# Level masks on VectorE, a residual loaded in eight pieces and a gate bank emptied by ScalarE, in a transformer trunk layer on one core

## The chip, the cores and the metric

The kernel runs on one core of one Trainium2 chip. The metric is the device time of one execution in microseconds (us); the number for a kernel is the median of several runs. Engines are named as in the profile: PE (TensorE), DVE (VectorE), ACT (ScalarE), POOL (GpSimd) and SP (SyncE, which issues the DMAs).

## The reference

One layer of a streaming encoder for two request groups, 256 + 64 = 320 tokens in all, width 2048:

```
h = rmsnorm(x);  p = h @ w_in                       # 2048 -> 6160 columns
a_out = conformer_conv(p[:, :2048])                 # GLU, depthwise conv of width 31, group norm, swish
b_out = gdn_mixer(p[:, 2048:])                      # 8 heads of gated delta rule, chunks of 64 tokens
x = x + rmsnorm(concat(a_out, b_out) @ w_out)
h = rmsnorm(x)
gu = causal_dwconv(h @ w_up)                        # 2048 -> 11264, width 3
x = x + rmsnorm((silu(gate) * up) @ w_down)         # 5632 -> 2048
```

The delta rule of a chunk needs the inverse of a triangular matrix `m + eye`:

```
m = where(strict, einsum('bhnid,bhnjd->bhnij', kb, k) * decay, 0.0)
tmat = triangular_solve(m + eye, eye, lower=True, unit_diagonal=True)
```

All of it is float32, and the states of the convolutions and of the delta rule are returned as well.

## The kernel before

Activations lie with channels on the 128 partitions and the 320 tokens in the free dimension. Every float32 operand of a large product is split into a high and a low part, and each weight tile gives three matmuls into one PSUM bank (high x high, high x low, low x high: L210, L211 and L214 of `block_matmul`). The weights are streamed: `load_split` has SP start the DMA of one piece of up to 128x1024 elements into one of three buffers `w`, ACT casts it into `whi` (L194), and DVE subtracts to get `wlo` (L195). There are three buffers each for `w`, `whi` and `wlo`, so a DMA starts when the piece three before it has been split.

PE runs the dense products as one long row, and everything else hangs on it. Small pieces of work are generators, called jobs: the gates, the tail of a convolution block, the tail of a head, and a pair of heads with its triangular inverse. `tick` is called after each dense matmul, and after every 20 it takes the jobs that are due in order and advances each by one step, as long as the PSUM banks of pool g (four banks) and pool t (two banks) that their steps ask for, summed within the tick, don't exceed 4 and 2. A step's instructions are then put behind that matmul; the framework's scheduler makes one fixed order for each engine out of this.

`levels` joins the inverse of 16-wide diagonal blocks (which `base_inverse` made) into 32-wide and then 64-wide blocks. It runs four times, once for each pair of heads, and has two masked levels, w=16 and w=32. N (tile `np`) is the factor; a level takes only its blocks right above the block diagonal. Before, POOL multiplies N by a 0/1 mask into `nm` (L720), PE forms `pz` from `nm` (L729), ACT copies `pz` to `zs` (L730), and PE forms `px` and `py` from `zs` (L734, L737), which DVE adds to the inverse `wtp` (L738, L739). This is done for all NI = 5 chunks of two heads at once, so the tiles have 128x640 (nm) or 128x320 (zs, px, py) elements.

`gates` empties the bank `psba` (the raw gates of the 8 heads, in pool p) with two DVE products with `rb`, the row of reciprocal norms (L398, L399). The bank is one of the two that the dense products alternate on.

After the mixer the second dense product with `w_out` runs in two parts; the last is a loop over 16 blocks n, each with one piece `w_out2[n]` of 320 KB, 15 matmuls and the sum of squares. The residual x is loaded into `x1` (2.56 MB, L932) ahead of this loop, followed by the parameters `fpar` (L933). `x1` is first read after the loop.

Of the kernel before, what the change touches and what calls it, by code (L numbers as in the profile page):

```python
# [9 lines left out]
F32 = mybir.dt.float32  # L10
F32R = mybir.dt.float32r
AF = mybir.ActivationFunctionType
ALU = mybir.AluOpType
# [4 lines left out]
P = 128  # L18
D = 2048
KB = D // P  # L20
TP = 256
TS = 64
# [57 lines left out]
def chunk_constants():  # L80
    i = np.arange(P)
    c = np.zeros((P, NCST), np.float32)

    def put(name, m):
        o, w = CST[name]
        c[:, o:o + w] = m

    put("ident", np.eye(P))
    put("tri", i[:, None] <= i[None, :])
    put("strict", i[:, None] > i[None, :])  # L90
    put("ones", 1.0)
    same = i[:, None] // TS == i[None, :] // TS
    put("tri2", same & (i[:, None] <= i[None, :]))
    put("strict2", same & (i[:, None] > i[None, :]))
    put("half", 0.5)
    for name, b in (("m16", 16), ("m32", 32)):
        r, q = i[:, None] // b, i[None, :] // b
        put(name, (r % 2 == 0) & (q == r + 1))
    return c


# [1 line left out]
def trunk_kernel(ctx, tc, ins, outs):  # L103
# [7 lines left out]


    dense = [None, 0]
    jobs = []


# [8 lines left out]
    def advance(job):  # L125
        with tc.issue_after(dense[0]), tc.high_priority(offset=PRI_J):
            try:
                wait, job[2], job[3] = next(job[1])
                job[0] = dense[1] + wait
            except StopIteration:  # L130
                jobs.remove(job)
# [10 lines left out]
    def tick(mm):  # L142
        dense[0] = mm.ins
        dense[1] += 1
        if dense[1] % GAP == 0:
            g = t = 0
            for job in sorted(jobs, key=lambda j: j[0]):
                if job[0] <= dense[1] and g + job[2] <= 4 and t + job[3] <= 2:
                    g += job[2]
                    t += job[3]  # L150
                    advance(job)
            for _ in range(min(pace[0], len(taps))):
                next_tap()

# [240 lines left out]

    def gates():
        baT = cb.tile([32, 3, P], F32, tag="un", bufs=1, name="baT").rearrange("p c f -> p (c f)")
        V.tensor_tensor(baT[:, 0:T], psba[0:32, 0:T], rb[0:32, :], ALU.mult)  # L398
        V.tensor_tensor(baT[:, T:T + TS], psba[0:32, TP:T], rb[0:32, TP:T], ALU.mult)  # L399
        ba = const.tile([P, 3, 16], F32, tag="ba", name="ba")  # L400
        yield LAG_WAIT, 0, 1
        pst = ps_t.tile([P, 512], F32, tag="t", name="pst_ba")
# [313 lines left out]
    def levels(st):  # L716
        N, W, TT = st["np"], st["w"][:, 0, :, :], st["w"][:, 1, :, :]
        for name, w in (("m16", 16), ("m32", 32)):
            nm = gd.tile([P, NI, P], F32, tag="nm", bufs=1, name="nm")
            G.tensor_tensor(nm, N, cv(name).unsqueeze(1).to_broadcast((P, NI, P)), ALU.mult)  # L720
            G.memset(halves(zs, 16, 1) if w == 16 else halves(zs, w, 1)[:, :, :, 0:16], 0.0)
            pz, px, py = [], [], []

            def out(name):
                return ps_g.tile([P, 512], F32, tag="g", name=name)[:, 0:NI * 64].rearrange("p (a b w) -> p a b w", a=NI, w=w)

            pz = out("pz")
            for a in range(NI):
                PE.matmul(pz[:, a], nm[:, a, :], halves(TT, w, 0)[:, a], start=True, stop=True)  # L729
            S.copy(halves(zs, w, 0), pz)  # L730
            yield LAG_WAIT, 2, 0
            px, py = out("px"), out("py")
            for a in range(NI):
                PE.matmul(px[:, a], zs[:, a, :], halves(W, w, 1)[:, a], start=True, stop=True)  # L734
            nt = NI if w == 16 else S_
            for a in range(nt):
                PE.matmul(py[:, a], W[:, a, :], halves(zs, w, 0)[:, a], start=True, stop=True)  # L737
            V.tensor_tensor(halves(W, w, 1), halves(W, w, 1), px, ALU.add)  # L738
            V.tensor_tensor(halves(TT, w, 0)[:, 0:nt], halves(TT, w, 0)[:, 0:nt], py[:, 0:nt], ALU.add)  # L739
            yield LAG_ADD, 1, 0  # L740
        pz = ps_g.tile([P, 512], F32, tag="g", name="pz")[:, 0:256].rearrange("p (a f) -> p a f", a=S_)
        for a in range(S_):
            PE.matmul(pz[:, a, :], N[:, a, :], TT[:, a, 0:64], start=True, stop=True)
        S.copy(zs[:, 0:S_, 0:64], pz)
        yield LAG_WAIT, 1, 0
        px = ps_g.tile([P, 512], F32, tag="g", name="px")[0:64, 0:256].rearrange("p (a f) -> p a f", a=S_)
        for a in range(S_):
            PE.matmul(px[:, a, :], zs[:, a, 0:64], W[:, a, 64:128], start=True, stop=True)
        S.copy(W[0:64, 0:S_, 64:128], px)
# [179 lines left out]
    x1 = res.tile([P, KB, T], F32, tag="x1", name="x1")  # L929
    fpar = res.tile([P, NFP], F32, tag="fpar", name="fpar")  # L930
    nffn = res.tile([P, 88, 2, 2], F32, tag="nffn", name="nffn")
    nc.sync.dma_start(x1, ins["x"])  # L932
    nc.sync.dma_start(fpar, ins["fpar"])  # L933
    acc = None

    def fv(name, a, b=None):
# [24 lines left out]
    for n in range(KB):  # L961
        hi, lo = load_split(ins["w_out2"][n], nk2 * P)
        if n in (4, 8):
            upw.append(up_weights(len(upw), ugp))
        whole = n == KB - 1
        psm = ps_p.tile([P, 512], F32, tag="p", name="psm2")
        if whole:
# [257 lines left out]
```

## Time and profile before

| | |
|---|---|
| median of 3 runs | 1529.96 us (1528.54 to 1530.36) |
| the profiled execution, its own time | 1527.28 us |
| its span, first to last instruction | 1525.2 us |
| mean granted TensorE clock | 0.997 of full speed |
| PE busy | 1502.0 us (98%), 10232 matmuls |
| DVE busy | 1009.9 us (66%) |
| ACT busy | 734.4 us (48%) |
| POOL busy | 303.6 us (20%) |
| DMA moved | 224.29 MB, mean 147 GB/s |

The profile is one execution, taken apart into instructions. Busy is the time in which an engine has an instruction in work; the rest of the span it waits. The times in the sections below count from the start of the span. The 2 us between span and own time lie before the first and after the last instruction.

### The profile page before, as it was taken

To read this page: it belongs to the slowest core of one execution; us is meant where nothing else is said; L and a number is where in the kernel's file an instruction comes from. 1 tells how busy PE (TensorE), PEld (TensorE's weight loads), DVE (VectorE), ACT (ScalarE), POOL (GpSimd) and SP (SyncE) were. 2 spreads that over 40 slices of the span, in tenths; PEclk is the share of its full clock that TensorE was granted. 3 is DMA by queue.
4 is the path that set the end of the run, shared out by engine and by line. 5 is a ranking of instruction groups with operands and counts; after the bars stand their busy time and mean duration, and the time that the engine had idled before them with its cause. 6 is when DMAs were issued, how large, how long until landed. Compare 5 with 4: busy or idle time off the path is not lost.

```text
span 1525.2 us, 26534 instructions
## 1 busy us (share of the span) xinstructions
PE 1502.0 (98%) x10232; PEld 1480.9 (97%) x10232; DVE 1009.9 (66%) x1841; ACT 734.4 (48%) x1215; POOL 303.6 (20%) x475
## 2 busy tenths in 40 slices
PE   9999999989999999999999999999999999999998
PEld 8999999989999989999999999999999999999997
DVE  6679797888997469766435665545666545666554
ACT  7674655545555565544334444333444333444453
POOL 0323233331110000332001322101222101222101
PEclk9999999999999999999999999999999999999999
DMA  8435443444434653444455455455544455444453
GB/s 297 129 112 159 143 142 110 119 146 119 132 101 138 202 169 125 140 151 144 134 152 168 150 153 149 126 151 170 153 152 149 128 152 167 151 152 152 127 151 116
DMA packets 95974, 224.29 MB, mean 147 GB/s; under 512 B 18536, under 2 KB 36968, under 8 KB 95720
## 3 DMA queue, kind: packets, MB, share of 16 engines
q1 hardware_dynamic: 95704, 222.57, 48.4%
q8 instruction: 80, 1.31, 0.4%
q14 instruction: 46, 0.38, 0.1%
q10 hardware_dynamic: 144, 0.03, 0.0%
HBM read 215.45 MB, written 7.12 MB: 146 GB/s over the span
## 4 chain that ended last, share of the span: by engine, by line
PE 86%; DVE 9%; ACT 1%; issue 1%; POOL 1%; DMA 1%; DVEq 0%; ACTq 0%; SPq 0%; POOLq 0%
PE psu L210 13%; PE psu L211 13%; PE psu L214 13%; PE psdn L210 7%; PE psdn L211 7%; PE psdn L214 7%; DVE cvt L513 3%; DVE wlo L195 3%; PE psq L210 2%; PE psq L211 2%; PE psq L214 2%; PE psm L214 1%; PE psm L211 1%; PE ps_first L372 1%; PE psm L210 1%
## 5 line engine op out<-in xcount | busy, mean ns | idle before, releaser
L194 ACT CAST whi<-w 128x1024 fp32r<-128x1024 f32 (+2 forms) x440 | 413.0, 940 | 509.0 <-PE psu L211 171.3
L195 DVE TENSOR_TENSOR wlo<-w,whi 128x1024 fp32r<-128x1024 f32 (+2 forms) x440 | 478.0, 1087 | 184.7 <-ACT whi L194 106.0
L210 PE MATMUL psu<-hi,whi 128*128 128x320 f32 x1344 | 397.0, 309 | 1.3 <-DVE fbuf L1062 1.3
L211 PE MATMUL psu<-lo,whi 128*128 128x320 f32 x1344 | 396.9, 309 | 0.0
L210 PEld LDWEIGHTS psu<-hi,whi 128*128 128x128 f32 x1344 | 252.3, 188 | 1.4 <-ACT rb L1044 1.4
L211 PEld LDWEIGHTS psu<-lo,whi 128*128 128x128 f32 x1344 | 252.3, 188 | 0.0
L214 PE MATMUL psu<-hi,wlo 128*128 128x320 f32 x1344 | 224.4, 309 | 0.0
L1063 POOL COPY nffn<-fbuf 128x2 f32<-128x2 f32 x88 | 101.4, 1153 | 588.4 <-DVE fbuf L1061 584.0
L211 PE MATMUL psdn<-gl,whi 128*128 128x320 f32 x704 | 208.9, 310 | 0.0
L214 PEld LDWEIGHTS psu<-hi,wlo 128*128 128x128 f32 x1344 | 204.1, 188 | 0.0
L210 PE MATMUL psdn<-gh,whi 128*128 128x320 f32 x512 | 152.3, 309 | 0.0
L1061 DVE TENSOR_TENSOR fbuf<-psu,rb 128x256 f32<-128x256 f32 x88 | 37.3, 424 | 169.8 <-PE psu L214 169.8
L513 DVE SCALAR_TENSOR_TENSOR cvt<-ub,par,cvt 128x350 f32<-128x350 f32 x240 | 141.1, 602 | 2.7 <-ACT cvt L512 0.3
L211 PEld LDWEIGHTS psdn<-gl,whi 128*128 128x128 f32 x704 | 132.2, 188 | 0.3
L210 PE MATMUL psq<-hh,whi 128*128 128x320 f32 x352 | 106.5, 316 | 1.2 <-DVE baT L399 1.2
L211 PE MATMUL psq<-hl,whi 128*128 128x320 f32 x352 | 104.1, 309 | 0.0
L210 PEld LDWEIGHTS psdn<-gh,whi 128*128 128x128 f32 x512 | 96.1, 188 | 0.0
L214 PE MATMUL psdn<-gh,wlo 128*128 128x320 f32 x512 | 95.8, 309 | 0.0
L214 PEld LDWEIGHTS psdn<-gh,wlo 128*128 128x128 f32 x512 | 80.4, 188 | 0.0
L210 PEld LDWEIGHTS psq<-hh,whi 128*128 128x128 f32 x352 | 66.1, 188 | 1.8 <-issue 1.6
L211 PEld LDWEIGHTS psq<-hl,whi 128*128 128x128 f32 x352 | 66.2, 188 | 0.3 <-issue 0.2
L1105 DVE TENSOR_TENSOR y<-y,psdn 128x320 f32<-128x320 f32 x48 | 23.4, 488 | 63.6 <-PE psdn L214 63.6
(328 smaller groups left out, 2514.0 us busy)
## 6 DMA issues: line engine op xcount, KB each, us to landing
w<-in_w_up SPq DMA_DIRECT2D x176, 512.0 KB, 3.7
w<-in_w_in SPq DMA_DIRECT2D x88, 512.0 KB, 3.7
w<-in_w_down SPq DMA_DIRECT2D x64, 384.0 KB, 3.0
w<-in_w_down SPq DMA_DIRECT2D x64, 320.0 KB, 2.8
w<-in_w_out SPq DMA_DIRECT2D x32, 320.0 KB, 2.9
w<-in_w_out SPq DMA_DIRECT2D x16, 384.0 KB
w<-in_w_first SPq DMA_DIRECT2D x6, 512.0 KB, 5.5
wtp<-wsp SPq DMA_DIRECT2D x4, 640.0 KB
```

What stands on the lines that cost most here:

```text
L194: S.copy(hi[:, 0:width], w[:, 0:width])
L195: V.tensor_tensor(lo[:, 0:width], w[:, 0:width], hi[:, 0:width].bitcast(F32), ALU.subtract)
L210: tick(PE.matmul(ps, wh, xh, start=(k0 + j == 0), stop=False))
L211: tick(PE.matmul(ps, wh, xl, start=False, stop=False))
L214: tick(PE.matmul(ps, lo[:, j * P:(j + 1) * P], xh, start=False, stop=(final and k0 + j == nk - 1)))
L372: tick(PE.matmul(ps, w, xh, start=(k == 0 and wt is hi), stop=(k == KB - 1 and wt is lo)))
L513: return lambda: V.scalar_tensor_tensor(cvt, ub[:, t:t + 350], pv("w_dw", b * 31 + t), cvt, ALU.mult, ALU.add)
L1061: V.tensor_tensor(buf[:, 2:258], psu[:, 0:TP], rb2[:, 0:TP], ALU.mult)
L1063: G.tensor_copy(nffn[:, b, 0, :], buf[:, 256:258])
L1105: V.tensor_tensor(y[:, n, :], y[:, n, :], psd[:, 0:T], ALU.add)
```

## The change

There are four edits. In `levels` the product on POOL goes away: PE multiplies the unmasked N, and DVE multiplies the product `pz` by the mask while it moves it to `zs`; ACT no longer copies it. The masks m16 and m32 are transposed for this. In `gates` two ACT copies take `psba` to SBUF at once, and one tick later DVE multiplies there by `rb`. In `tick` the pool-t banks asked for in the previous tick count against the limit too (`held_t`). And the residual is loaded in eight pieces of 320 KB, one in each of the first eight passes of the `w_out2` loop, with `fpar` in the tenth.

```diff
--- before.py
+++ after.py
@@ -95,7 +95,7 @@
     put("half", 0.5)
     for name, b in (("m16", 16), ("m32", 32)):
         r, q = i[:, None] // b, i[None, :] // b
-        put(name, (r % 2 == 0) & (q == r + 1))
+        put(name, (q % 2 == 0) & (r == q + 1))
     return c
 
 
@@ -111,6 +111,7 @@
 
 
     dense = [None, 0]
+    held_t = [0]
     jobs = []
 
 
@@ -143,12 +144,14 @@
         dense[0] = mm.ins
         dense[1] += 1
         if dense[1] % GAP == 0:
-            g = t = 0
+            g, t0 = 0, held_t[0]
+            t = t0
             for job in sorted(jobs, key=lambda j: j[0]):
                 if job[0] <= dense[1] and g + job[2] <= 4 and t + job[3] <= 2:
                     g += job[2]
                     t += job[3]
                     advance(job)
+            held_t[0] = t - t0
             for _ in range(min(pace[0], len(taps))):
                 next_tap()
 
@@ -395,8 +398,11 @@
 
     def gates():
         baT = cb.tile([32, 3, P], F32, tag="un", bufs=1, name="baT").rearrange("p c f -> p (c f)")
-        V.tensor_tensor(baT[:, 0:T], psba[0:32, 0:T], rb[0:32, :], ALU.mult)
-        V.tensor_tensor(baT[:, T:T + TS], psba[0:32, TP:T], rb[0:32, TP:T], ALU.mult)
+        S.copy(baT[:, 0:T], psba[0:32, 0:T])
+        S.copy(baT[:, T:T + TS], psba[0:32, TP:T])
+        yield 1, 0, 0
+        V.tensor_tensor(baT[:, 0:T], baT[:, 0:T], rb[0:32, :], ALU.mult)
+        V.tensor_tensor(baT[:, T:T + TS], baT[:, T:T + TS], rb[0:32, TP:T], ALU.mult)
         ba = const.tile([P, 3, 16], F32, tag="ba", name="ba")
         yield LAG_WAIT, 0, 1
         pst = ps_t.tile([P, 512], F32, tag="t", name="pst_ba")
@@ -716,8 +722,6 @@
     def levels(st):
         N, W, TT = st["np"], st["w"][:, 0, :, :], st["w"][:, 1, :, :]
         for name, w in (("m16", 16), ("m32", 32)):
-            nm = gd.tile([P, NI, P], F32, tag="nm", bufs=1, name="nm")
-            G.tensor_tensor(nm, N, cv(name).unsqueeze(1).to_broadcast((P, NI, P)), ALU.mult)
             G.memset(halves(zs, 16, 1) if w == 16 else halves(zs, w, 1)[:, :, :, 0:16], 0.0)
             pz, px, py = [], [], []
 
@@ -726,8 +730,9 @@
 
             pz = out("pz")
             for a in range(NI):
-                PE.matmul(pz[:, a], nm[:, a, :], halves(TT, w, 0)[:, a], start=True, stop=True)
-            S.copy(halves(zs, w, 0), pz)
+                PE.matmul(pz[:, a], N[:, a, :], halves(TT, w, 0)[:, a], start=True, stop=True)
+            mask = cv(name).rearrange("p (b e w) -> p b e w", e=2, w=w)[:, :, 0, :]
+            V.tensor_tensor(halves(zs, w, 0), pz, mask.unsqueeze(1).to_broadcast((P, NI, P // 2 // w, w)), ALU.mult)
             yield LAG_WAIT, 2, 0
             px, py = out("px"), out("py")
             for a in range(NI):
@@ -929,8 +934,6 @@
     x1 = res.tile([P, KB, T], F32, tag="x1", name="x1")
     fpar = res.tile([P, NFP], F32, tag="fpar", name="fpar")
     nffn = res.tile([P, 88, 2, 2], F32, tag="nffn", name="nffn")
-    nc.sync.dma_start(x1, ins["x"])
-    nc.sync.dma_start(fpar, ins["fpar"])
     acc = None
 
     def fv(name, a, b=None):
@@ -962,6 +965,10 @@
         hi, lo = load_split(ins["w_out2"][n], nk2 * P)
         if n in (4, 8):
             upw.append(up_weights(len(upw), ugp))
+        if n < 8:
+            nc.sync.dma_start(x1[:, 2 * n:2 * n + 2, :], ins["x"][:, 2 * n:2 * n + 2, :])
+        elif n == 9:
+            nc.sync.dma_start(fpar, ins["fpar"])
         whole = n == KB - 1
         psm = ps_p.tile([P, 512], F32, tag="p", name="psm2")
         if whole:
```

The first place is DVE's order at pair 2's first level (w=16), some 326 us into the span. `gnm` belongs to a convolution's group norm, `cq` and `cvt` are accumulations of the short and the wide convolution. Before:

```order
L581 SCALAR_TENSOR_TENSOR cq<-qb_595,par,cq 128x323
L536 SCALAR_TENSOR_TENSOR gnm<-gvar,grs 128x3
L195 TENSOR_TENSOR wlo<-w,whi 128x1024
L581 SCALAR_TENSOR_TENSOR cq<-qb_595,par,cq 128x323
L513 SCALAR_TENSOR_TENSOR cvt<-ub_588,par,cvt 128x350
L195 TENSOR_TENSOR wlo<-w,whi 128x1024
L513 SCALAR_TENSOR_TENSOR cvt<-ub_588,par,cvt 128x350 x4
L738 TENSOR_TENSOR wtp<-wtp,px 128x20x16
L739 TENSOR_TENSOR wtp<-wtp,py 128x20x16
```

After the change (lines count three to six more there):

```order
L587 SCALAR_TENSOR_TENSOR cq<-qb_595,par,cq 128x323
L542 SCALAR_TENSOR_TENSOR gnm<-gvar,grs 128x3
L198 TENSOR_TENSOR wlo<-w,whi 128x1024
L587 SCALAR_TENSOR_TENSOR cq<-qb_595,par,cq 128x323
L735 TENSOR_TENSOR zs<-pz,cst 128x20x16
L198 TENSOR_TENSOR wlo<-w,whi 128x1024
L519 SCALAR_TENSOR_TENSOR cvt<-ub_588,par,cvt 128x350 x4
L743 TENSOR_TENSOR wtp<-wtp,px 128x20x16
L744 TENSOR_TENSOR wtp<-wtp,py 128x20x16
```

The product into `zs` now stands on DVE behind `gnm`, one `wlo` and one `cq`; one `cvt` that stood among them has moved down. On ACT the copy stood behind the `un` that `gnm` releases, two activations on `cq` (`vT`, `vts`) and a third `un`. Before, ACT had there:

```order
L539 ACTIVATE un<-pt_c,gnm,grs 128x128 x2
L582 ACTIVATE vT<-cq 128x256
L583 ACTIVATE vts<-cq 128x64
L539 ACTIVATE un<-pt_c,gnm,grs 128x128
L730 COPY zs<-pz 128x20x16
L194 CAST whi<-w 128x1024
```

The row `zs<-pz` is the one that has left ACT.

The second place is SP's queue of DMA issues at the residual load. Before, with `x_6072` the residual:

```order
L187 DMA w<-in_w_out 128x640 x6
L932 DMA x_6072<-in_x 128x5120
L187 DMA w<-in_w_up 128x4x256
L187 DMA w<-in_w_out 128x640 x2
L933 DMA fpar<-in_fpar 128x528
L187 DMA w<-in_w_out 128x640 x2
L187 DMA w<-in_w_up 128x4x256
L187 DMA w<-in_w_out 128x640 x7
```

After the change, where `x_6058` is the residual:

```order
L190 DMA w<-in_w_out 128x640 x6
L969 DMA x_6058<-in_x 128x640
L190 DMA w<-in_w_up 128x4x256
L969 DMA x_6058<-in_x 128x640 x2
L190 DMA w<-in_w_out 128x640
L969 DMA x_6058<-in_x 128x640
L190 DMA w<-in_w_out 128x640 x2
L969 DMA x_6058<-in_x 128x640
L190 DMA w<-in_w_out 128x640
L969 DMA x_6058<-in_x 128x640
L190 DMA w<-in_w_up 128x4x256
L190 DMA w<-in_w_out 128x640
```

The one large issue has become eight, which stand between the pieces of `w_out2`; the second piece of `w_up` has moved up among them, and the last two pieces of the residual and then `fpar` follow below these rows.

The third place is PE's order some 474 us into the span, where a convolution's second transposes (`pt_c<-cst,un`) take a bank of pool t that `pt_o` held. `psm` is the dense product. Before, 20 rows stand between `pt_o` and `pt_c`, and the last of them are:

```order
L214 MATMUL psm<-bh_4638,wlo 128x320
L214 MATMUL psm<-bh_5085,wlo 128x320
L214 MATMUL psm<-bp_2707,wlo 128x320
L210 MATMUL psm<-bp_2707,whi 128x320
L543 MATMUL pt_c_5512<-cst,un 128x128 x3
L211 MATMUL psm<-bl_2717,whi 128x320
```

After the change 38 rows stand between them, and the last are:

```order
L214 MATMUL psm<-bl_2270,whi 128x320
L213 MATMUL psm<-bh_3146,whi 128x320
L214 MATMUL psm<-bl_3147,whi 128x320
L213 MATMUL psm<-bh_4090,whi 128x320
L214 MATMUL psm<-bl_4091,whi 128x320
L549 MATMUL pt_c_5531<-cst,un 128x128 x3
L213 MATMUL psm<-bh_4628,whi 128x320
```

The transposes have moved down by 18 dense matmuls.

## Rows read from the trace of the kernel before

**Rows 1.** Windows: length, busy us (instructions) by engine, PEclk, DMA share, GB/s.

```profile
0.00:20.00 20.00, 18.66 (x103) 15.56 (x104) 13.19 (x20) 15.68 (x25) 2.50 (x7) 1.00 0.92 326
320.00:340.00 20.00, 14.80 (x88) 14.53 (x87) 16.02 (x32) 7.76 (x14) 3.78 (x7) 0.83 0.34 102
400.00:440.00 40.00, 39.33 (x293) 38.73 (x292) 38.38 (x71) 19.23 (x31) 5.12 (x6) 1.00 0.35 103
640.00:1500.00 860.00, 860.00 (x5858) 858.91 (x5857) 485.92 (x786) 367.93 (x487) 155.86 (x237) 1.00 0.50 149
```

**Rows 2.** Waits of PE, whole span: us in total, times, longest.

```profile
PE px L734 <- ACT zs L730: 5.9, 2, 5.2
...
PE pt_c L543 <- DVE zo L860: 2.0, 1, 2.0
...
PE psm L211 <- DVE bl L219: 1.1, 1, 1.1
...
PE psm L972 <- ACT whi L194: 0.5, 1, 0.5
```

**Rows 3.** Timeline at 326 us: start, us, engine, line, out<-in, count [idle <-releaser].

```profile
327.36 1.53 POOL L720 TENSOR_TENSOR nm<-np,cst 128x640 f32<-128x640 f32 x1
...
327.42 1.49 DVE L536 SCALAR_TENSOR_TENSOR gnm<-gvar,grs 128x3 f32<-128x3 f32 x1 [1.09 <-POOL grs L534]
...
328.83 1.21 DVE L195 TENSOR_TENSOR wlo<-w,whi 128x1024 fp32r<-128x1024 f32 x1
...
329.97 0.54 DVE L581 SCALAR_TENSOR_TENSOR cq<-qb,par,cq 128x323 f32<-128x323 f32 x1
...
331.36 0.41 ACT L730 COPY zs<-pz 128x320 f32<-128x320 f32 x1
...
331.82 2.40 PE L734 MATMUL px<-wtp,zs 128*128 128x64 f32 x10 [5.20 <-ACT zs L730]
...
334.01 2.34 PE L737 MATMUL py<-zs,wtp 128*128 128x64 f32 x10
...
336.11 2.38 PE L214 MATMUL psgate<-hh,wlo 128*128 128x320 f32 x8
```

**Rows 4.** Timeline elsewhere: the same PE work and the same gnm.

```profile
164.15 1.28 PE L737 MATMUL py<-zs,wtp 128*128 128x64 f32 x10
...
424.31 0.16 DVE L536 SCALAR_TENSOR_TENSOR gnm<-gvar,grs 128x3 f32<-128x3 f32 x1 [1.02 <-POOL grs L534]
```

**Rows 5.** Groups by line and form: busy, mean ns | idle before, releaser.

```profile
L720 POOL TENSOR_TENSOR nm<-np,cst 128x640 f32<-128x640 f32 x8 | 13.8, 1726 | 14.4 <-PE pz L729 7.6 <-DVE np L665 6.8
...
L738 DVE TENSOR_TENSOR wtp<-wtp,px 128x320 f32<-128x320 f32 x8 | 3.8, 478 | 4.4 <-PE py L737 4.4
```

**Rows 6.** Timeline at the emptying of the gate bank.

```profile
40.81 0.32 PE L285 MATMUL psba<-hl,wbz 128*128 128x320 f32 x1
...
47.49 1.33 PE L214 MATMUL psq<-hh,wlo 128*128 128x320 f32 x8
...
49.98 0.39 PE L210 MATMUL psq<-hh,whi 128*128 128x320 f32 x1 [1.16 <-DVE baT L399]
```

**Rows 7.** Timeline at the residual load.

```profile
523.86 0.33 SPq L932 DMA_DIRECT2D x<-in_x  x1
...
534.09 1.05 ACT L194 CAST whi<-w 128x1024 fp32r<-128x1024 f32 x1
...
536.41 0.41 PE L972 MATMUL psm<-bh,whi 128*128 128x320 f32 x1 [1.70 <-DVE wlo L195]
```

**Rows 8.** Windows while the residual landed, columns as in rows 1.

```profile
526.00:534.00 8.00, 8.00 (x57) 8.00 (x56) 4.88 (x9) 5.14 (x10) 0.00 (x0) 1.00 0.98 398
```

**Rows 9.** DMA issues of the page: KB each, us to landing.

```profile
w<-in_w_out SPq DMA_DIRECT2D x32, 320.0 KB, 2.9
```

**Rows 10.** Timeline at pair 3's first level.

```profile
404.61 1.81 DVE L513 SCALAR_TENSOR_TENSOR cvt<-ub,par,cvt 128x350 f32<-128x350 f32 x3
...
405.22 1.22 PE L734 MATMUL px<-wtp,zs 128*128 128x64 f32 x10
```

## The prediction

> **What bounds the kernel now.** I read the windows first. From 640 to 1500 us PE is busy in all 860 of 860 us [rows 1]: the change has nothing to win there, and all of its gain must come from the first third of the span and the stretch around the residual load. In the window from 320 to 340 PE is busy for only 14.80 us, and its granted clock is 0.83 [rows 1]: that is the one place ahead of the tail where the clock falls. The waits of PE say what stops it [rows 2]: `px` waits 5.9 us in all for ACT's `zs`, 5.2 of it at once; `pt_c` waits 2.0 for DVE's `zo`; `psm` waits 1.1 for DVE's `bl` and 0.5 for a cast. Two more stand in the timelines: 1.16 for DVE's `baT` [rows 6], and 1.70 at the residual load [rows 7]. Every one of these is touched by the change, and together they are 11 us plus the slower clock. So the question is not whether the edits aim at waits, but how much of each wait comes back.
>
> **The mask: the wait at 326 us.** In the timeline of pair 2's first level [rows 3] read backwards from `px` at 331.82. ACT's copy to `zs` runs at 331.36, behind activations that wait for `gnm` and `cq` of DVE. DVE's `gnm`, an instruction on 128x3 elements, begins at 327.42 and takes 1.49 us; the same `gnm` takes 0.16 at 424.31 [rows 4]. The difference, 1.33 us, lies exactly beside POOL's `nm` (327.36, 1.53 us). So POOL's product holds up a DVE instruction that reads two operands from SBUF, and that product is removed.
>
> After the change `zs` is DVE's, behind `gnm`, a `wlo` and a `cq`. I walk these from the rows: `wlo` starts 1.33 earlier than 328.83, at 327.50; `cq` 1.33 earlier than 329.97, at 328.64, and ends at 329.18; `zs` then takes about what the nearest row of its kind takes, a DVE addition of a PSUM bank of 128x320 to SBUF, 478 ns [rows 5]. So `zs` is done at 329.66, and `px` starts near 329.7 instead of 331.82: 2.1 us come back. Pair 2's other `nm` product goes as well, and if it holds DVE up by another 1.33 at a time when DVE has no slack, up to 3.4 come back; nothing less than 2.1 does unless the DVE queue grows. I take 2.5, nearer the walk. A wait of about 2.7 stays.
>
> **The mask: the clock at 326 us.** Behind the wait of 5.20 us PE runs at a lower clock: `px` and `py`, ten matmuls each, take 2.40 and 2.34 us, and the eight of `psgate` behind them 2.38 [rows 3]. The same `py` takes 1.28 at 164.15 [rows 4], and eight matmuls of that form 1.33 at 47.49 [rows 6]. The loss is 2.40 + 2.34 - 2 x 1.28 = 2.2, and 2.38 - 1.33 = 1.0, so 3.2 us. The window's 0.83 agrees: 17% of 20 us, 3.4. After the residual load's wait of 1.70 the clock was not lost, nor after the 2.0 of `pt_c`: the windows show it in this one place only. A wait of 2.7 lies between 2.0, where it stays at 2.4 GHz, and 5.2, where it goes to 1.2; being nearer to the first, I take all 3.2, with 0 as the other bound.
>
> **The mask: the rest.** DVE gains eight `zs` of 0.48 us, 3.8 us in all, and loses what `nm` costs it. POOL's eight products take 1.73 us each [rows 5]; where DVE stands beside one with two SBUF operands it can lose up to 1.33, eight times 10.6 at the most. Either way DVE is not loaded more than before by more than 3.8 us. That matters because DVE is busy 38.38 of 40 us between 400 and 440 [rows 1]. At pair 3's first level `px` starts at 405.22 without a wait, while DVE runs three `cvt` from 404.61 to 406.42 [rows 10]; a `zs` that stands inside such a run comes some 0.3 to 0.6 us late. I give back 0.4 there, and allow 1.4 for all the other small leads of weight pieces that the earlier PE eats into (0.5 at each of three places, estimated from `zs`' own 0.48). ACT loses eight short copies, and it is not what PE waits for; they are worth nothing.
>
> **The gate bank.** The last product into it ends at 41.13, and PE needs the bank again after the eight matmuls at 47.49, that is at 48.82, but starts at 49.98, having waited 1.16 [rows 6]: DVE's products stand behind others that need `rb`. The two ACT copies need no `rb`, and have over seven us for less than one (the copy of 128x320 on ACT takes 0.41 [rows 3]). The whole 1.2 comes back.
>
> **The limit on pool-t banks.** `pt_c` moves down by 18 matmuls. At 0.15 us each that is 2.6 us, more than the wait of 2.0, so the bank is free when PE comes to it. But DVE loses the breath that the wait gave it, and what reads `pt_c` moves down as well. I take 1.6, between 0 and 2.0. The `bl` of the 1.1 us wait comes a little earlier on DVE: 0.6, between 0 and 1.1.
>
> **The residual.** The single load begins at 523.86 on SP's queue [rows 7], and from 526 to 534 the queues run at 398 GB/s [rows 8]; the pieces of weights behind it land late: the next cast is at 534.09, and PE waits 1.70 to 536.41 [rows 7], and then 0.5 more [rows 2]. In eight pieces each pass of the loop asks for 320 KB of weights and 320 KB of residual, 655 KB. A pass has 15 matmuls, 2.2 us. So the demand is 298 GB/s, under the 398 shown here and the 326 that the start of the kernel sustains [rows 1]. I take all of 1.7 + 0.5 = 2.2, between 0 and 2.2.
>
> The Trainium skill's page "DMA: Bandwidth & Descriptors" (section "Bandwidth", the measured table's rule) speaks against this edit: batch DMAs to at least 1 MiB, since smaller ones don't reach three quarters of the peak; and its section "Anatomy of one DMA" gives a fixed cost of about 2.0 us a DMA. By its fit one load of 2.6 MB is about 8 us and eight of 320 KB are 22, an estimate, 14 more. The trace does not agree that pieces run one behind the other: at the start of the kernel, where x and the first weights come in pieces too, 326 GB/s were moved [rows 1].
>
> **The sum.** 1.2 + 2.5 + 3.2 + 0.6 + 1.6 + 2.2 = 11.3, less 1.8 given back, is 9.5 us. The profiled execution took 1527.28 us, so 1517.8 by its measure. The median of before is 1529.96, 2.7 above that execution; on it the same gain gives 1520.5.
>
> **The rivals.** *The clock falls again.* A wait of 2.7 may be long enough. Then the 3.2 are not won: 1523.7. For it speaks that nothing between 2.0 and 5.2 has been seen.
>
> *DVE takes the gain back.* From 400 to 440 DVE is nearly full [rows 1], and a stretch that DVE limits ends when DVE does, however early PE arrives. Then the gains ahead of it, 1.2 + 2.5 + 3.2 = 6.9, vanish, and the time is 1527.4. Against it: DVE's work follows PE's products, and can start earlier with them.
>
> *`zs` becomes the late one (slower).* ACT had room for the copy; DVE's queue in pairs 2 and 3 is full, with `wlo` of 1.21 and three `cvt` of 1.81 us ahead [rows 3, 10]. If `zs` waits behind 1.2 + 1.8 = 3.1 us at the three other levels of these pairs and at pair 2's first nothing is won in its walk, it is 3 x 3.1 + 2.5 above the forecast: 1532.3. It decides as soon as `px` waits over 3 us at two levels. Against it: the order puts `zs` behind a few rows only, and in front of most `cvt`.
>
> *Eight pieces run one after another.* A piece of 320 KB takes 2.9 us from issue to landing [rows 9]. If one piece of weights and one of residual landed in turn, a pass would take 5.8 instead of 2.2, eight times 3.6 = 29, less the lead of three buffers, 6.6; with the 2.2 not won it is 24 above the forecast, 1545. This is what the page's rule would do at its worst. Against it stand the 398 GB/s.
>
> **How the numbers follow.** Forecast 0.50, its own range 1517 to 1523.5 (all bounds won; the residual and 1 us more lost); clock 0.15; given back 0.14; `zs` late 0.08; pieces in turn 0.04; better than the forecast's range 0.09. This kernel's measurement tells 0.2%, 3 us, from no change, so faster is under 1526.9: 0.50 + 0.15 + 0.09 = 0.74; same 0.14; slower 0.12. The range reaches from 1516 to 1528: it leaves out the two slow cases and part of the best.
>
> **What the profile would show.** Right: no wait of `psq` for `baT`; no POOL product, and a `gnm` of 0.16 us at 326; `px` there waits near 2.7 us for DVE's `zs`, with the granted clock of 320 to 340 at 1.00; `pt_c` without a wait at 474; no wait of `psm` for weights at 536. Wrong: a window with a clock under 1, `px` waiting at several levels, or casts in the `w_out2` loop that wait for their DMA. What would upset all of it is a new wait in the stretch from 395 to 480, where DVE is late already.

## The result and the profile after

The changed kernel takes 1519.71 us (median of 4 runs, 1519.58 to 1520.18), the kernel before 1529.84 in runs beside it (4 runs, 1528.54 to 1530.36). The ratio is 0.9936 with a 95% interval of 0.9918 to 0.9953: it is faster by 0.5 to 0.8%. The forecast was 1520.5, with a range of 1516 to 1528.

The profiled executions differ by less than the medians do. After, span 1517.6 and own time 1520.18; before, 1525.2 and 1527.28. That is 7.6 us of span and 7.1 of own time against 10.1 us of median, and the difference is a finding of its own (below).

Answering to [rows 2], these are waits of PE in the changed kernel (us in total, times, longest):

```profile
PE px L739 <- DVE zs L735: 3.1, 2, 2.5
...
PE psm L979 <- DVE m L987: 1.2, 1, 1.2
...
PE pks L663 <- ACT vh L655: 1.0, 1, 1.0
...
PE psm L213 <- ACT whi L197: 1.0, 2, 0.7
...
PE psm L979 <- ACT whi L197: 0.9, 1, 0.9
```

Gone are `psq` for `baT`, `psm` for `bl` and `pt_c` for `zo`. The wait of `px` is 3.1 instead of 5.9. New or longer are a wait of `psm` for a sum `m` on DVE, `pks` for ACT (0.7 before, now 1.0), and `psm` for casts at three places, 455, 486 and 526 us.

Answering to [rows 1], windows of the changed kernel, with the stretch of the residual load as the third:

```profile
320.00:340.00 20.00, 17.46 (x109) 17.21 (x108) 14.79 (x32) 8.50 (x23) 4.97 (x10) 0.83 0.36 109
400.00:440.00 40.00, 39.40 (x295) 38.79 (x294) 38.40 (x74) 19.68 (x36) 3.62 (x5) 1.00 0.31 95
518.00:526.00 8.00, 7.89 (x54) 7.62 (x52) 4.17 (x7) 4.42 (x7) 0.00 (x0) 1.00 0.89 288
640.00:1500.00 860.00, 860.00 (x5858) 858.90 (x5857) 483.31 (x779) 367.10 (x486) 154.10 (x233) 1.00 0.49 148
```

PE is as full from 640 on as before, and the gain is all in front of it, as it had to be. PE has 17.46 of the 20 us from 320 to 340 instead of 14.80, but the granted clock of that window is 0.83 once more. DVE between 400 and 440 is as full as it was.

Answering to [rows 3], the timeline at pair 2's first level:

```profile
324.96 0.16 DVE L542 SCALAR_TENSOR_TENSOR gnm<-gvar,grs 128x3 f32<-128x3 f32 x1 [1.09 <-POOL grs L540]
...
325.04 1.22 DVE L198 TENSOR_TENSOR wlo<-w,whi 128x1024 fp32r<-128x1024 f32 x1
...
326.17 0.55 DVE L587 SCALAR_TENSOR_TENSOR cq<-qb,par,cq 128x323 f32<-128x323 f32 x1
...
326.64 0.48 DVE L735 TENSOR_TENSOR zs<-pz,cst 128x320 f32<-128x320 f32 x1
...
327.26 2.37 PE L739 MATMUL px<-wtp,zs 128*128 128x64 f32 x10 [2.54 <-DVE zs L735]
...
329.43 2.34 PE L742 MATMUL py<-zs,wtp 128*128 128x64 f32 x10
...
331.53 2.48 PE L217 MATMUL psgate<-hh,wlo 128*128 128x320 f32 x8
```

`gnm` takes 0.16 us, nothing stands on POOL beside it, and `zs` on DVE takes 0.48. PE's wait is 2.54. But `px`, `py` and the eight `psgate` run at 2.37, 2.34 and 2.48 us, as slowly as before, against 1.28 for the ten and 1.33 for the eight at full clock [rows 4, 6].

Answering to [rows 7], the stretch of the residual in eight pieces:

```profile
523.49 1.05 ACT L197 CAST whi<-w 128x1024 fp32r<-128x1024 f32 x1 [1.38 <-DMA w<-in_w_up]
...
526.01 0.72 ACT L197 CAST whi<-w 128x640 fp32r<-128x640 f32 x1 [0.50 <-DMA w<-in_w_out]
...
526.74 0.39 PE L979 MATMUL psm<-bh,whi 128*128 128x320 f32 x1 [0.85 <-ACT whi L197]
...
535.14 1.68 ACT L197 CAST whi<-w 128x1024 fp32r<-128x1024 f32 x2 [1.26 <-DMA w<-in_w_up]
...
538.50 0.48 DVE L987 TENSOR_TENSOR m<-m,psm 128x320 f32<-128x320 f32 x1
...
539.13 0.38 PE L979 MATMUL psm<-bh,whi 128*128 128x320 f32 x1 [1.16 <-DVE m L987]
```

ACT's cast of a piece of `w_up` (L197, 128x1024) comes late because its DMA lands late; what stands behind it on ACT and DVE is late with it, and PE waits twice: 0.85 for a cast, 1.16 for DVE's sum `m`, which frees a bank. So 2.0 us of new waits stand where 1.7 and 0.5 stood.

Of the 7.6 us of span, the waits that can be named on both sides come to 6.2: gate bank 1.16, a gate wait of 0.3 behind it, `px` 2.66 in pair 2 and 0.07 net in pair 3, `bl` 1.06, `pt_c` 1.96 and the residual 0.22, less 0.34, 0.30 and 0.66 for the longer waits of `pks` and of casts at 455 and 486. That is all of PE's idle time: span less PE's busy time is 23.2 us before and 17.0 after. The other 1.4 us are PE's busy time (1502.0 before, 1500.6 after), and I did not assign them to rows.

### The profile page after: what moved, and what is told of

The parts are those of the page before. It is cut to its first block, busy times and chain, and to the rows that moved or that the text cites. A ratio compares the mean times of both kernels' runs of the same rounds, so it can differ in the third digit from the quotient of the medians.

```text
span 1517.6 us, 26528 instructions
## 1 busy us (share of the span) xinstructions
PE 1500.6 (99%) x10231; PEld 1480.4 (98%) x10232; DVE 1007.1 (66%) x1849; ACT 732.4 (48%) x1209; POOL 286.9 (19%) x467
## 4 chain that ended last, share of the span: by engine, by line
PE 90%; DVE 6%; ACT 1%; POOL 1%; issue 1%; DMA 1%; ACTq 0%; DVEq 0%; POOLq 0%
PE psu L213 13%; PE psu L214 13%; PE psu L217 13%; PE psdn L213 7%; PE psdn L214 7%; PE psdn L217 7%; PE psq L217 3%; PE psq L213 3%; PE psq L214 3%; DVE wlo L198 2%; DVE cvt L519 2%; PE ps_first L375 1%; PE psu L1034 1%; PE psm L213 1%; PE psm L214 1%; PE psv L217 1%
## 5 line engine op out<-in xcount | busy, mean ns | idle before, releaser
L197 ACT CAST whi<-w 128x1024 fp32r<-128x1024 f32 (+2 forms) x440 | 412.5, 940 | 515.5 <-PE psu L214 167.1
L519 DVE SCALAR_TENSOR_TENSOR cvt<-ub,par,cvt 128x350 f32<-128x350 f32 x240 | 137.4, 588 | 2.7 <-ACT cvt L518 0.3
```

The source lines that it names most:

```text
L197: S.copy(hi[:, 0:width], w[:, 0:width])
L519: return lambda: V.scalar_tensor_tensor(cvt, ub[:, t:t + 350], pv("w_dw", b * 31 + t), cvt, ALU.mult, ALU.add)
```

## The experiments

### The four edits one by one

Each edit of the change was put into the kernel before alone. The cores of the four diffs, in this order, are:

```diff
 # p1_mask (with the masks transposed)
-            G.tensor_tensor(nm, N, cv(name).unsqueeze(1).to_broadcast((P, NI, P)), ALU.mult)
-                PE.matmul(pz[:, a], nm[:, a, :], halves(TT, w, 0)[:, a], start=True, stop=True)
-            S.copy(halves(zs, w, 0), pz)
+                PE.matmul(pz[:, a], N[:, a, :], halves(TT, w, 0)[:, a], start=True, stop=True)
+            V.tensor_tensor(halves(zs, w, 0), pz, mask.unsqueeze(1).to_broadcast((P, NI, P // 2 // w, w)), ALU.mult)
 # p2_gate
-        V.tensor_tensor(baT[:, 0:T], psba[0:32, 0:T], rb[0:32, :], ALU.mult)
+        S.copy(baT[:, 0:T], psba[0:32, 0:T])
+        yield 1, 0, 0
+        V.tensor_tensor(baT[:, 0:T], baT[:, 0:T], rb[0:32, :], ALU.mult)
 # p3_held
-            g = t = 0
+            g, t0 = 0, held_t[0]
+            t = t0
+            held_t[0] = t - t0
 # p4_pieces
-    nc.sync.dma_start(x1, ins["x"])
+        if n < 8:
+            nc.sync.dma_start(x1[:, 2 * n:2 * n + 2, :], ins["x"][:, 2 * n:2 * n + 2, :])
```

> The kernel before with the mask edit alone (DVE masks pz, no product on POOL). Theory A (waits as read from the two traces): the wait of px in pair 2 goes from 5.2 to about 2.5 us, the clock still falls behind it, the other levels change by a few tenths; 2.5 to 3 us less than before, about 1527. Theory B (the mask edit is what lightens DVE, and the waits of 1.1 and 2.0 us at 445 and 474 went with it): about 6 us less, 1524.

> The kernel before with the gate bank emptied by ACT alone. Theory A: the 1.16 us wait of psq at 49 goes and stays won, 1.2 us less, about 1528.6. Theory B: DVE between 280 and 480 takes it back, no change (within 0.3 us).

> The kernel before with the limit on pool-t banks alone. Theory A: it moves the transposes at 474 and the bl at 445, and both waits go, 2.0 + 1.1 = about 3 us less, 1526.8. Theory B: those two waits went because DVE has less to do, and this edit alone changes nothing there: within 0.5 us of before.

> The kernel before with the residual in eight pieces alone. Theory A: the waits of 1.7 and 0.5 us go and new ones of about 0.9 and 1.2 us (a cast that waits for its piece of weights, then DVE's sum of m behind a split) take their place: 0.2 us less, no change to be measured. Theory B: the new waits come from the other edits, and alone the edit wins its 2.2 us: about 1527.6.

Measured beside 1528.28 us of before (27 runs, 1526.88 to 1531.5):

| edit alone | median us | less than before | ratio, 95% interval |
|---|---|---|---|
| mask on DVE | 1522.39 | 5.9 | 0.996 (0.9946 to 0.9974) |
| gate bank by ACT | 1526.27 | 2.0 | 0.9985 (0.9976 to 0.9993) |
| limit on pool-t banks | 1528.32 | 0.0 | 0.9996 (0.9987 to 1.0004) |
| residual in pieces | 1526.08 | 2.2 | 0.9983 (0.9974 to 0.9992) |

The four differences add up to 10.1, which is what the whole change gave beside its own runs of before. Each interval is 1 us wide or more to either side, so that they agree to a tenth is chance. Where they come from is not what the two profiles above suggest, so the waits of each edit matter.

**The mask alone.** Theory A is wrong by a factor of two; B has the size but not all of the reason. Waits of PE with the mask edit alone:

```profile
PE px L733 <- DVE zs L729: 3.1, 2, 2.4
...
PE psm L971 <- ACT whi L194: 2.2, 2, 1.7
...
PE pt_c L543 <- DVE zo L859: 1.8, 1, 1.8
```

The `px` wait is 2.4 in pair 2, as in the whole change. The wait for DVE's `bl` is gone too; DVE's busy time is 1007.1 us here, against 1009.9 before. The 1.8 of `pt_c` stays, which B had wrong. The last part is in the clock. Windows of this kernel, the second at the residual load:

```profile
320.00:345.00 25.00, 22.58 (x154) 22.09 (x153) 19.82 (x42) 13.39 (x34) 5.33 (x12) 0.93 0.37 110
525.00:545.00 20.00, 17.79 (x108) 17.09 (x107) 13.74 (x23) 13.07 (x23) 2.02 (x4) 0.91 0.68 212
```

At 320 to 345 the clock is 0.93; the kernel before has 0.86 in the same window in its profile, and 7% of 25 us are 1.8. The waits give 2.8 for `px`, 1.1 for `bl` and 0.2 for `pt_c`, 4.1 in all, and PE's idle time fell by as much (23.2 to 19.1 us). The 1.8 can't be added to reach 5.9: the second window's 0.91 is a loss of the same size that the first profile of before does not have, and the two profiles differ by 5.2 us of span. What the medians show beyond 4.1 fits the mean granted clock of the runs, 0.996 or 0.997 in the five of this kernel and 0.994 to 0.996 in 22 of the 27 of before. The stretch is not of one length either: the changed kernel has 0.86 behind the same wait, and two kernels with the long wait, below, have 0.80. The second window is taken up below.

**The gate bank alone** is theory A. The wait of 1.16 is gone, and with it one of 0.33 for the gate tile `gt` at 72 us; that is 1.5 of the 2.0, whose interval reaches from 1.1 to 3.7.

**The limit alone** changes nothing that the medians can tell (the interval reaches from 0.6 more to 2.0 less), so B's outcome holds, but not its reason: the two waits do go, and others come. Waits of PE:

```profile
PE psm L213 <- ACT whi L197: 1.1, 2, 0.7
...
PE pks L660 <- ACT vh L652: 1.0, 1, 1.0
...
PE pvns L808 <- DVE rhs L800: 0.3, 1, 0.3
...
PE pz L732 <- DVE wtp L742: 0.2, 1, 0.2
```

No `pt_c` and no `bl`, 3.0 us less; but `pks` at 1.0, `pvns` and `pz` with 0.3 and 0.2, and 1.1 in two waits for casts, which is 2.0 more than before. The 1.0 that is left lies inside the interval.

**The residual in pieces alone** wins 2.2, which is B's number. Its reason is wrong: the waits that were to come from the other edits are there without them. The new wait of PE, and the clock there:

```profile
PE psm L974 <- DVE m L982: 1.5, 2, 1.2
```

```profile
525.00:545.00 20.00, 18.51 (x125) 18.04 (x124) 14.43 (x24) 14.70 (x25) 0.07 (x1) 1.00 0.92 306
```

With 1.5 us in place of 1.7 and 0.5, the waits give only 0.7. The clock from 525 to 545 is 1.00. It is 1.00 in all seven profiles with the pieces. In the gate kernel, which has the single load, it isn't:

```profile
320.00:345.00 25.00, 20.14 (x123) 19.87 (x122) 17.43 (x34) 10.33 (x30) 6.84 (x13) 0.80 0.29 88
525.00:545.00 20.00, 17.68 (x110) 17.16 (x109) 12.83 (x22) 12.98 (x23) 1.86 (x4) 0.91 0.75 270
```

Here the second window has 0.91, so 9% of 20 us, 1.8, are lost around the load's wait of 1.8 us; and the first window has 0.80, worse than the 0.86 of the first profile, behind a `px` wait that is no longer than there (4.9). The limit kernel shows 0.80 and 0.91 as well, the mask kernel 0.91 in the second window. The profile that the prediction was made from had 0.86 and 1.00: what the residual's wait costs beside itself does not show in it.

### The single load put back, the limit taken out, and the kernel before once more

```diff
 # r2_after_one_load, from the changed kernel
+    nc.sync.dma_start(x1, ins["x"])
+    nc.sync.dma_start(fpar, ins["fpar"])
-        if n < 8:
-            nc.sync.dma_start(x1[:, 2 * n:2 * n + 2, :], ins["x"][:, 2 * n:2 * n + 2, :])
 # r3_after_no_limit, from the changed kernel
-            g, t0 = 0, held_t[0]
+            g = t = 0
```

> The changed kernel with the residual in one load again, all else kept. Theory A (alone the pieces won 2.2 us, most of it a slow stretch of the clock behind the 1.7 us wait): the waits of 1.7 and 0.5 come back and in some runs the slow stretch, 1521.5 to 1522.5. Theory B (read from the waits of the two profiles alone, 2.2 against 2.0): within 0.5 us of the changed kernel.

> The changed kernel without the limit on pool-t banks. Theory A (alone it gave nothing: the wait of 2.0 at 474 went, and others of 0.3 to 0.7 at 112, 455 and 486 came): about the same as the changed kernel, 1519 to 1520.5. Theory B (it wins the 2.0 where DVE is lighter): 1521.3 to 1522.

> The kernel before, once more. Theory A (the stretch of lower clock differs from run to run): the same waits of 5.2 and 1.7 us, but a slow stretch of another length behind the first, or one behind the second too, and a time up to 3 us above the first profile's 1527.3. Theory B: the same stretches as in the first profile and the time differs before the first or behind the last instruction.

With one load: 1522.3 us (4 runs, 1521.87 to 1523.05), ratio to before 0.9957 (0.994 to 0.9973), 2.6 more than the changed kernel. Theory A holds. The waits are 2.2 and the clock of the second window is 0.91:

```profile
PE psm L977 <- ACT whi L197: 2.2, 2, 1.7
```

```profile
525.00:545.00 20.00, 17.78 (x109) 17.25 (x108) 13.71 (x23) 13.52 (x24) 2.02 (x4) 0.91 0.70 216
```

Without the limit: 1519.91 us (1516.94 to 1521.13), ratio 0.9937 (0.9922 to 0.9951), the same as with it. `pt_c` waits for `zo` again, and nothing is lost by it: A holds.

```profile
PE pt_c L546 <- DVE zo L862: 1.8, 1, 1.8
```

The kernel before once more: 1527.13 us, in a single execution, and beside it 1528.76 in 7 runs (1528.14 to 1530.65). Its windows:

```profile
320.00:345.00 25.00, 20.09 (x128) 19.82 (x127) 18.50 (x36) 10.64 (x30) 6.84 (x13) 0.86 0.31 96
525.00:545.00 20.00, 17.78 (x120) 17.26 (x119) 12.78 (x21) 13.48 (x23) 2.00 (x4) 1.00 0.77 276
```

They are those of the first profile, 0.86 and 1.00, and so is the time, within 0.2 us. So theory A did not show itself here: two executions of before at 1527.1 and 1527.3 have one slow stretch. But each run is on record with its span and its mean granted clock. Of the 46 runs of before beside the experiments, six have 0.997, as both profiled executions have, with spans of 1524.7 to 1526.0 us; the other 40 have 0.994 to 0.996, with spans of 1525.6 to 1529.1. So the longer runs are those that spent more time at a lower clock. Where in the span is not shown, since no longer run of before was profiled; a longer stretch at 326 or a second one at the residual is what the gate and the limit kernel make likely, which run the same work at both places.

### The wait of px taken away

```diff
-            yield LAG_WAIT, 2, 0
+            yield LAG_WAIT + (GAP if st['i'] == 2 and w == 16 else 0), 2, 0
```

This puts `px` and `py` of pair 2's first level 20 dense matmuls later, in the changed kernel; in the kernel before, with `2 * GAP`, 40.

> The changed kernel with px of pair 2's first level put one tick (20 dense matmuls, 2.9 us) later. Theory A (the lower clock is the wait's): the 2.54 us wait at 324 goes, the clock stays at 1.00 there, and the loss of 3.2 us with it: 5 to 6 us less than the changed kernel, about 1514. Theory B (the clock falls there for another cause, such as what px and py do, or the work moved takes the gain back behind 400 us): the wait goes but the clock still falls, or a later wait grows: 2.5 us less at most, about 1517.5 or above.

> The kernel before with px of pair 2's first level put two ticks (40 dense matmuls, 5.9 us) later, and the POOL product kept. Theory A (of the mask edit's gain, the wait of px is the larger part): the wait of 5.2 and the slow stretch go, 5 to 9 us less than before, 1519 to 1523. Theory B (POOL's product holds up DVE all along the pairs and DVE gives the end of the stretch at 480): the time won at 326 returns as waits between 400 and 480, 1526 or above.

Changed kernel: 1519.16 us (4 runs, 1517.65 to 1519.57), ratio to before 0.9941 (0.9924 to 0.9957). Waits of PE, and windows:

```profile
PE px L739 <- DVE zs L735: 2.4, 1, 2.4
```

```profile
320.00:345.00 25.00, 25.00 (x187) 24.83 (x187) 18.70 (x40) 14.99 (x36) 6.22 (x12) 1.00 0.45 132
395.00:425.00 30.00, 27.57 (x194) 27.33 (x194) 27.78 (x55) 11.90 (x17) 3.35 (x5) 0.94 0.35 108
```

The wait at 324 is gone, and so is the slow stretch: 320 to 345 has a clock of 1.00 and PE is busy for all 25 us. So the lower clock there comes with the wait. But pair 3's `px` now waits 2.4 for `zs` instead of 0.6, at 398, and there the clock is 0.94 over 30 us, which is 1.8 us; a cast and a product (`pvn`) add 0.3. Of some 5.8 us won in front (2.5 of wait, 3.3 of clock), 4 come back behind: part of A, part of B. By the two profiles 2.0 us of span are left, by the medians 0.6.

Kernel before: 1524.62 us (9 runs, 1522.65 to 1526.58), ratio 0.997 (0.996 to 0.998), 4.7 less than its 1529.36 beside it and between the two theories. The wait of 5.2 is gone as well, and waits came in other places:

```profile
PE pk L653 <- ACT vh L649: 2.1, 1, 2.1
...
PE px L734 <- ACT zs L730: 1.2, 1, 1.2
```

The wait of `pk` ends at 341, that of `px` at 413. The clock behind them:

```profile
335.00:350.00 15.00, 12.93 (x92) 12.36 (x90) 12.34 (x26) 10.07 (x26) 4.88 (x9) 1.00 0.44 130
410.00:425.00 15.00, 13.79 (x92) 13.56 (x91) 13.87 (x32) 8.64 (x14) 1.12 (x2) 0.89 0.36 107
```

Behind the wait of 2.1 it stays at 1.00, and behind that of 1.2 it falls. So the length of a wait alone does not tell whether the clock falls.

By the medians nearly half of the whole change's gain (4.7 of 10.1) could be had at this place without touching the mask.

```diff
-            yield LAG_WAIT, 2, 0
+            yield LAG_WAIT + (GAP if st['i'] > 1 and w == 16 else 0), 2, 0
-        if n in (4, 8):
+        if n in (10, 13):
```

The last kernel moves `px` in pair 3 as well, and the two pieces of `w_up` behind those of the residual; `q4_after_up_late` has the second edit alone.

> The changed kernel with px of the first level one tick later in pairs 2 and 3, and w_up's two pieces in passes 10 and 13. Theory A (a wait moved off PE stays off where DVE has slack behind it): the waits at 324 and 398 go, with both slow stretches, and of the two at the residual half a microsecond stays; 1514 to 1516. Theory B (pairs 2 and 3 are limited by DVE, so what is won in front comes back as a wait behind 400): another wait of 2 to 3 us between 400 and 490, 1518 to 1519.

> The changed kernel with the two pieces of w_up loaded in passes 10 and 13 of the w_out2 loop instead of 4 and 8, so that they stand behind the pieces of the residual. Theory A (the waits of 0.85 and 1.16 us at 526 and 538 come from w_up's pieces between those of the residual: ACT's cast of w_up waits for its DMA and what follows it is late): both waits go, 2 us less, about 1517.7. Theory B (the queue is simply full while the residual comes in): the waits stay or move by some passes, within 0.7 us of the changed kernel.

Both `px` later: 1518.59 us (4 runs, 1516.67 to 1519.28), ratio 0.9929 (0.9914 to 0.9944). Theory B: `px` now waits 2.7 at pair 3's second level. On DVE and the clock there:

```profile
413.84 0.16 DVE L542 SCALAR_TENSOR_TENSOR gnm<-gvar,grs 128x3 f32<-128x3 f32 x1 [1.09 <-POOL grs L540]
...
415.95 0.48 DVE L735 TENSOR_TENSOR zs<-pz,cst 128x320 f32<-128x320 f32 x1
```

```profile
395.00:425.00 30.00, 27.26 (x180) 27.02 (x180) 26.98 (x53) 10.02 (x15) 3.30 (x5) 0.89 0.34 100
```

`zs` comes at 415.95 on a DVE that waited once, 1.09 us for POOL ahead of `gnm`, and was busy with other work right up to it. The clock of this window is 0.89. Three kernels, three places (324, 398, 413), and a wait between 2.4 and 2.7 in each: in these three PE waits for DVE somewhere in this stretch, and putting `px` later only moved the place.

`w_up` later alone: 1519.12 us (1516.78 to 1520.76), ratio 0.9938 (0.9924 to 0.9953). Its waits:

```profile
PE pst L236 <- DVE acc L952: 0.6, 1, 0.6
...
PE psm L979 <- DVE m L987: 0.4, 1, 0.4
```

Of 2.0 us at the residual 0.4 and 0.6 are left, so about 1 us is won by the waits; the medians differ by 0.6 with ranges that overlap, so A and B are not told apart by the time.

### POOL's product kept

```diff
+            nm = gd.tile([P, NI, P], F32, tag="nm", bufs=1, name="nm")
+            G.tensor_tensor(nm, N, cv(name).unsqueeze(1).to_broadcast((P, NI, P)), ALU.mult)
```

In the changed kernel, with `nm` read by nobody.

> The changed kernel with POOL's product into nm done as before, its result read by nobody. Theory A (POOL's product holds up DVE's instruction beside it): gnm at 325 takes 1.5 instead of 0.16 us, px there waits 1.3 longer (3.8 to 3.9 us), and DVE between 400 and 440 loses another 1.3: 1521.5 to 1524. Theory B (the gain is ACT's copy that left its queue behind un and vT): gnm still short, no change, 1519.7 within 0.5.

1522.2 us (4 runs, 1520.8 to 1525.25), ratio 0.9962 (0.9948 to 0.9977): by the medians 2.5 more than without it, by the profiles 1.2 of span. The time is A's, but the place is another. Since nobody reads `nm`, the two products of a pair run one after the other at its start, and `gnm` stays short; so this kernel does not repeat what held `gnm` up at 326. That shows across the runs: `gnm` there takes 1.49 to 1.55 us in the six profiles with an `nm` beside it, and 0.16 in the eight without. At pair 2's start, and then at its `px`:

```profile
279.51 3.43 POOL L726 TENSOR_TENSOR nm<-np,cst 128x640 f32<-128x640 f32 x2 [0.81 <-DVE np L671]
...
280.25 3.07 DVE L519 SCALAR_TENSOR_TENSOR cvt<-ub,par,cvt 128x350 f32<-128x350 f32 x2
...
329.01 2.37 PE L741 MATMUL px<-wtp,zs 128*128 128x64 f32 x10 [4.06 <-DVE zs L737]
```

The same two `cvt` in the changed kernel, and in the kernel before, which has one `nm` there (281.18, 1.60 us):

```profile
280.00 1.20 DVE L519 SCALAR_TENSOR_TENSOR cvt<-ub,par,cvt 128x350 f32<-128x350 f32 x2
...
281.92 1.86 DVE L513 SCALAR_TENSOR_TENSOR cvt<-ub,par,cvt 128x350 f32<-128x350 f32 x2
```

They take 3.07 us beside two products, 1.86 beside one and 1.20 without, so 1.87 and 0.66 more. `px` at 324 waits 4.06 instead of 2.54, and no other `nm` runs between. That POOL's product with two SBUF operands holds up DVE's instruction with two SBUF operands is shown; that the delay at 281 is the one that arrives at 324 fits the numbers, 1.87 there and 1.5 here. Holding up DVE is what the Trainium skill states on its page "SBUF — State Buffer" (section "Who interferes with whom"): a DVE instruction with two SBUF inputs and a GpSimd instruction that reads SBUF contend, and the one issued later waits. The trace agrees, with these numbers.

A second path adds to it. In pair 1 the two products keep POOL itself busy, so that POOL's `grs`, which releases `gnm` and with it `zs`, is late, and `px` has a wait that the changed kernel does not have:

```profile
168.70 3.23 POOL L726 TENSOR_TENSOR nm<-np,cst 128x640 f32<-128x640 f32 x2 [5.62 <-DVE np L671]
...
175.14 1.30 PE L741 MATMUL px<-wtp,zs 128*128 128x64 f32 x10 [0.77 <-DVE zs L737]
```

How much of the mask edit's gain comes from POOL's product and how much from the copy that left ACT's queue, no run separates.

## Why the prediction was right, and where it was not

**The total** is off by 0.8 us, and the range held: 9.5 us were forecast, the medians give 10.1. But the sum is better than its steps, and in part that is luck. Measured by the two profiles, as it was made, the gain is 7.6 of span and 7.1 of own time, since the slow stretch at 326 stayed; the medians give more mainly because most runs of before (40 of 46) have a lower mean clock than the profiled one; the median of their spans is 1526.8 against its 1525.2. Of the signs named for being right four came (`psq`, `gnm`, `px` and `pt_c`); the clock of 1.00 and the `w_out2` loop without waits did not. All three signs named for being wrong can be found: a window with a clock under 1, `px` waiting at two levels, and casts that wait for their DMA. Two sums are slightly off, and nothing hangs on them: the waits called 11 us at the start add up to 12.4, and the 3.1 of the slower rival, 1.2 + 1.8, is 3.0.

**Right: the gate bank.** Forecast 1.2, and the wait of 1.16 is gone; 2.0 alone by the medians, with an interval of 1.1 to 3.7.

**Right: the walk at 326 us.** `gnm` at 0.16, `zs` at 0.48, and a wait of 2.54 where 2.7 was to stay. The part of the 2.5 that went beyond the walk's 2.1 was for pair 2's first `nm`; it lengthened the two `cvt` beside it by 0.66, and the wait fell by 2.66.

**Wrong: the clock at 326 us.** The step was that a wait of 2.7, being nearer to 2.0 than to 5.2, leaves the clock at 2.4 GHz, worth 3.2. It does not: behind 2.54 us it is at half, as the rival with 0.15 had it; in all eleven profiles with a wait of 2.3 to 5.2 there, before and after, the clock falls. What failed is the reading of one execution as a scale of lengths. The 1.7 at the residual left the clock at 1.00 in that profile, and four others with a wait of 1.7 to 1.9 have 0.91; at `pt_c` the clock is 1.00 behind 1.8 to 2.1 in all seven profiles that have that wait; and a wait of 1.2 lost it in the kernel before with `px` later. Length alone did not decide it, and the 3.2 was not won in the changed kernel's profile. By the medians the mask alone gives 1.8 beyond its waits (5.9 less 4.1), so part of the term may have been won in other runs; no profile shows it.

**Right in size by another cause: the residual.** Forecast 2.2; 2.2 alone, 2.6 when undone. The step that pieces at 298 GB/s fit under 398 failed: in pieces the queues were busy for 0.89 of the time from 518 to 526 and moved 288 GB/s, where the single load had 0.98 and 398 [rows 8], and weights came late. Waits of 2.0 replaced 2.2 in the changed kernel, and 1.5 in the kernel with this edit alone. The demand of 298 also left out the two pieces of `w_up`, 512 KB each, that SP issues among the eight of the residual; with them it is 357 GB/s, an estimate from 6.3 MB in eight passes of 2.2 us. In the kernel that loads them later, 1.0 us of the waits is left. What the pieces won beyond the waits is, by the profiles, the slow stretch of about 1.8 us around the single load's wait, which the prediction had ruled out: it stands in four of the seven profiles with the single load and in none of the seven with pieces. The rule of the Trainium skill's page "DMA: Bandwidth & Descriptors" (section "Bandwidth") that spoke against small pieces was measured for DMAs issued from GpSimd; here, where SP issues them, it has this much in it, that the same share of the queues moved less. Eight pieces in turn, 24 us, did not happen.

**Mis-sized: the limit, 1.6.** By the medians it is worth 0.0 alone, with an interval that does not quite exclude 1.6, and 0.2 when undone. Both waits went, but what the jobs lost in time arrived as waits at `pks`, `pvns`, `pz` and casts. The `bl` of 0.6, put to the same edit, was all of 1.1, and the mask edit alone removes it.

**The give-back of 1.8** was 0.60 at pair 3's first level for a forecast of 0.4, less 0.67 that went at its second, and 1.3 in the three longer waits: 1.2 in sum, and the 1.3 is the limit's doing, since the kernel with the limit alone has these waits and the one without it does not.

**DVE takes the gain back** was not what happened to the change, but it is what happened to the next step: with the wait at 326 removed, it came back at 398, then at 413. That rival's place was right, and its 0.14 was for the wrong kernel.

**The slower rivals** fell: `zs` on DVE made `px` wait at two levels, 0.6 and 2.5, and never 3.1.

## What to carry to other kernels

A wait of the bounding engine costs more than its length if the clock falls behind it, and neither the wait's length nor one profile tells how often that is: look at the same wait in several executions before a stretch of lower clock is called won or ruled out. Before a job is made cheaper, look whether it can be put later: 20 or 40 matmuls of delay removed the same wait that the mask edit halved, until the engine behind it was full. And try each part alone: an edit that removes a wait of 2 us can be worth nothing.

## What the runs showed of the hardware

The granted clock after like waits differs from execution to execution. Behind `px` waits of 4.9 to 5.2 us the window from 320 to 345 has 0.86 in three executions and 0.80 in two, behind 2.3 to 2.5 it has 0.86 in four and 0.93 in one; around the single load's wait of 1.7 to 2.0 the window from 525 to 545 has 1.00 in three and 0.91 in four. This goes with the spread of the times: the 46 runs of before lie between 1526.88 and 1531.93 us, with mean granted clocks of 0.997 down to 0.994, and the four of the changed kernel between 1519.58 and 1520.18, all at 0.997.

In one execution the clock stayed at 1.00 behind a wait of 2.1 us (341 us) and fell behind one of 1.2 (413 us).

A pair of DVE instructions of 0.6 us each was held up for 1.87 us by two POOL products beside it, and for 0.66 by one; a DVE instruction on 128x3 elements took 1.49 to 1.55 us beside one, and 0.16 without.

While a load of 2560 KB in one DMA ran with weights beside it, the queues moved 398 GB/s at a share of 0.98; with the load in eight DMAs they moved 288 at 0.89 in the changed kernel, and 321 at 0.95 in the kernel with that edit alone (526 to 534 us).
